# Moving the low parts of split weights and the sums of x from GpSimd to VectorE, and giving a projection's second block more PSUM banks

## The chip, the cores and the metric

The kernel runs on one core of a Trainium2 chip. The metric is the device time of one execution in microseconds. A core has five engines that each work through a queue of their own in order: TensorE (PE) multiplies matrices, VectorE (DVE), ScalarE (ACT) and GpSimd (POOL) work element by element, and SyncE (SP) issues most transfers. SBUF is the memory on the core, and matrix products land in eight PSUM banks.

## The reference, cut to what matters

The reference is one inference step of a two-layer decoder over 1024 prompt tokens and 64 sample tokens, 1024 features, all in fp32. Layer 0 mixes by retention, layer 1 by dilated window attention, and both attend to a memory as well. After the mixer of each layer:

```python
xp = deepnorm_residual(xp, mix_p @ w_out[l], ln_mix_g[l], ln_mix_b[l])
xp = deepnorm_residual(xp, swiglu_ffn(xp, w_ffn_in[l], w_ffn_out[l]), ln_ffn_g[l], ln_ffn_b[l])

def deepnorm_residual(x, h, g, b):
    return layer_norm(ALPHA * x + h, g, b)

def swiglu_ffn(x, w_in, w_out):
    gate, up = jnp.split(x @ w_in, 2, axis=-1)          # 2 x 2816 columns
    return (jax.nn.silu(gate) * up) @ w_out
```

The sample tokens go through the same lines. The change lies in the projection by `w_out` and in the FFN.

## The kernel before

**Products from halves.** Each fp32 operand is held as a high part `h` (rounded to the matrix unit's fp32r by ScalarE) and a low part `l = x - h` (a subtraction). A product is three matmuls: high by low, low by high, high by high. `halves` (L232) makes both parts of a weight piece: `acopy` (L149) on ScalarE writes `wh`, `tt` (L152) on VectorE or GpSimd writes `wl`. L149 and L152 are the lines of nearly all element-wise work in the profile, so groups are told apart by the tiles they write.

**Weights.** `plan` lists all weights in the order of use. `load_raw` fetches an entry to `raw` or `rawu` tiles by SP, two entries ahead; `emit_piece` (L237) cuts it into pieces and splits them. A ring of six `wh`/`wl` tiles holds the pieces ahead. Entries of the FFN's input (`sf`) hold a gate and an up column block of 128 (one f) and give seven pieces; entries of the FFN's output (`fo`) and of the projection (`wo`) give two each, whose lows GpSimd makes.

**Gate units.** The FFN runs over tokens in two blocks (0 to 511, and 512 to 1087), and in each over 22 f. A unit, one f, is a Strassen-like scheme with seven products instead of eight: `gates` (L746) multiplies the seven weight pieces with seven sums of x (`XH`, `XL`), in the order 0, 4, 2, 1, 3, 5, 6. Four banks `A_`, `B_`, `C_`, `D_` take them, and VectorE reads them into `v` and `up`, multiplies with ScalarE's SiLU and writes the low part of `hid`; ScalarE writes `hid`'s high part. The weight pieces need sums as well, on VectorE: `s` (gate minus up rows), `rawu` and two that overwrite `raw`. After every four f (three in the last two groups) the `fo` products of that group follow, read by VectorE into `mx`.

```python
            eng = nc.vector if j in SFD else nc.gpsimd      # SFD = (2, 6)
```

**Sums of x.** `combine_x` (L700) makes the seven sums, `x11`, `t2`, `t3`, `t1`, `x21`, `t4`, `x22`, and splits each with `put`. Of the seven lows GpSimd makes the first, third and fifth (`PUT`), and it makes the sum `t3x`. For block 1 they are made in one step of all four k (1152 columns), after the last gates of block 0, while the last `fo` products of block 0 run.

**Projection.** `out_proj` (L659) runs over two blocks; block 1 has eight m with two chunks of tokens (256 and 320), each product in one of three banks of the pool `pd`, read by VectorE at L683. The other pool, `pa`, has four banks, which the norms and the attention use.

**Order.** The code emits instructions in the order of the text, with background generators (`Streams`, `S.tick`) in between; a scheduler of the framework then sets each engine's order, so the lines of one unit are interleaved with those of others.

Of the kernel before, what the change touches and what calls it, by code (L numbers as in the profile page):

```python
# [8 lines left out]
F32 = mybir.dt.float32  # L9
F32R = mybir.dt.float32r  # L10
AF = mybir.ActivationFunctionType
ALU = mybir.AluOpType
AX = mybir.AxisListType

P = 128
# [72 lines left out]
def trunk(ctx: ExitStack, tc: tile.TileContext, A: dict, O: dict, g128, g8):  # L88
    nc = tc.nc
# [18 lines left out]
    TK = ((3,), (2, 5), (1, 3, 5), (4,))  # L108
    BG = (120, 126, 128)
    PA = (6, 4)  # L110
    PUT = (1, 3, 5)
    WIN_ = (5, 4)
    SR = (2, 1)
    SY = (2, 3)
# [1 line left out]
    done = set()  # L116
# [13 lines left out]
    def slot(shape, dt=F32, name="slot"):  # L130
        return slots.tile(shape, dt, tag="slot", name=name)

    def rt(shape, name="rt"):
        return tp.tile(shape, F32, tag="rt", name=name)

    def bank(name="bank"):
        return pa.tile([P, 512], F32, tag="pa", name=name)

    def dbank(name="pd"):
        return pd.tile([P, 512], F32, tag="pd", name=name)  # L140
# [7 lines left out]
    def acopy(out, in_, scale=1.0):  # L148
        nc.scalar.activation(out, in_, AF.Copy, scale=scale)  # L149

    def tt(out, a, b, op, eng=None):
        (eng or nc.vector).tensor_tensor(out=out, in0=a, in1=b, op=op)  # L152
# [22 lines left out]


    WI, WB, WKV = A["w_in_a"][0], A["w_in_b"][0], A["w_kv_shared"]
    SFD = (2, 6)
    UNITS = ((2, 0), (1, 0), (0, 0), (2, 1), (1, 1), (0, 1))
    plan = []  # L180

# [50 lines left out]
    def halves(src, kt, eng):  # L232

        wh = wsp.tile([P, 4, P], F32R, tag="wh", name="wh")[:, :kt]
        wl = wsp.tile([P, 4, P], F32R, tag="wl", name="wl")[:, :kt]
        acopy(wh, src)
        tt(wl, src, wh.bitcast(F32), ALU.subtract, eng)  # L237
        return wh, wl

    def emit_piece():  # L240
# [6 lines left out]
        if key[0] == "sf":  # L247
            k4 = lambda t: t.rearrange("p (k m) -> p k m", m=P)
            g1, g2, u1, u2 = (k4(t[:, o:o + 512]) for t in r[:2] for o in (0, 512))
            eng = nc.vector if j in SFD else nc.gpsimd  # L250
            if j == 0:
# [45 lines left out]
    def weights(key, ahead=None, keep=False):  # L297

        assert plan[at["next"]][0] == key, (plan[at["next"]][0], key)
        at["next"] += 1  # L300
        if not keep:
            for w in held:
                w.clear()
            held.clear()
        held.append([piece(1), piece(PA[1] if ahead is None else ahead)])
        return held[-1]

    def dense(out, w, rhs, kt=KT):

        for k in range(kt):  # L310
            rh, rl = rhs(k)
            wh, wl = (t[:, k % 4, :] for t in w[k // 4])
            mm(out, lhsT=wl, rhs=rh, start=(k == 0), stop=False)  # L313
            mm(out, lhsT=wh, rhs=rl, start=False, stop=False)  # L314
            mm(out, lhsT=wh, rhs=rh, start=False, stop=(k == kt - 1))  # L315
            if k in S.at and kt == KT:
                S.tick()
# [337 lines left out]
    def out_proj(l, ready):  # L655
        for blk in range(2):
            S.at = TK[2] if l and blk == 0 else TK[3]
            S.until(lambda: all(k in done for c in BCH[blk] for k in ready(c)), blk if l else 1)
            b0, bn = BLK[blk][0][0], sum(n for _, n in BLK[blk])  # L659
            bs = slice(b0, b0 + bn)  # L660
            parts = []
            for k in range(KT):
                if blk == 0 and k > 1:
                    h, lo = xh[:, k - 2, bs], xl[:, k - 2, bs]
                elif k % 2 == 0:
                    hs, ls = (slot([P, 2, bn], F32R, nm) for nm in ("mixh", "mixl"))
                    h, lo = hs[:, 0], ls[:, 0]
                else:
                    h, lo = hs[:, 1], ls[:, 1]
                acopy(h, mx[:, k, bs])  # L670
                tt(lo, mx[:, k, bs], h.bitcast(F32), ALU.subtract)
                parts.append((h, lo))
                tt(mx[:, k, bs], xhf[:, k, bs], xlf[:, k, bs], ALU.add, nc.gpsimd if blk else nc.vector)
            done.add(("moved", l, blk))
            sums = [None, None]
            for m in range(KT):
                w = weights(("wo", l, blk, m))
                for i, c in enumerate(BCH[blk]):
                    c0, n = CH[c]
                    ps = dbank()[:, :n]  # L680
                    dense(ps, w, lambda k: tuple(t[:, c0 - b0:c0 - b0 + n] for t in parts[k]))
                    y = mx[:, m, c0:c0 + n]
                    nc.vector.scalar_tensor_tensor(out=y, in0=y, scalar=ALPHA, in1=ps, op0=ALU.mult, op1=ALU.add)  # L683
                    sums[i] = stat_add(sums[i], m, c, nc.vector)
                    S.tick()
            for i, c in enumerate(BCH[blk]):
                S.add(norm(c, sums[i], 0, l), level=2)
            S.add(combine_x(l, blk), level=2)


# [9 lines left out]
    def combine_x(l, blk):  # L700

        yield from wait(*[("ln", 0, l, c) for c in BCH[blk]], ("gates", l, 0) if blk else ("moved", l, 1))
        c0, n = HALF[blk]
        XH, XL = x_sums(blk)
        kk = 4 if blk else 2
        tmp = (lambda nm: slot([P, 4, n], F32, nm)) if blk else (lambda nm: rt([P, 2, n], nm))
        for k in range(0, 4, kk):
            x11, x12, x21, x22 = (mx[:, o + k:o + k + kk, t:t + n] for o in (0, 4) for t in (c0, c0 + n))
            turn = [0]

            def put(i, src):
                acopy(XH[:, i, k:k + kk], src)
                turn[0] += 1
                tt(XL[:, i, k:k + kk], src, XH[:, i, k:k + kk].bitcast(F32), ALU.subtract, nc.gpsimd if turn[0] in PUT else nc.vector)

            put(0, x11)
            t1 = tmp("t1x")
            tt(t1, x12, x11, ALU.subtract)
            t2 = tmp("t2x")
            tt(t2, x22, t1, ALU.subtract)  # L720
            put(4, t2)
            yield 1
            t3 = tmp("t3x")
            tt(t3, x22, x12, ALU.subtract, nc.gpsimd)
            put(2, t3)
            put(1, t1)
            yield 1
            put(3, x21)
            t4 = tmp("t4x")
            tt(t4, x21, t2, ALU.subtract)  # L730
            yield 1
            put(5, t4)
            put(6, x22)
            yield 1
        done.add(("xsum", l, blk))
# [9 lines left out]
    def ffn(l, background):  # L745
        def gates(blk, f, last):  # L746

            n = HALF[blk][1]
            XH, XL = x_sums(blk)
            assert plan[at["next"]][0] == ("sf", l, blk, f)  # L750
            at["next"] += 1

            def prod(i, ps, start, stop):
                wh, wl = piece(PA[0])
                for k in range(4):
                    mm(ps, lhsT=wl[:, k], rhs=XH[:, i, k], start=start and k == 0, stop=False, skip_group_check=True)  # L756
                    mm(ps, lhsT=wh[:, k], rhs=XL[:, i, k], start=False, stop=False, skip_group_check=True)  # L757
                    mm(ps, lhsT=wh[:, k], rhs=XH[:, i, k], start=False, stop=stop and k == 3, skip_group_check=True)  # L758
                S.tick()
                return ps  # L760

            sets["use"] ^= 1
            A_, B_, C_, D_ = (new_bank(i)[:, :n] for i in range(4))
            v, u1, u0 = (rt([P, n], nm) for nm in ("v1", "up1", "up0"))
            hid = slot([P, 2, 2 * n], F32R, "hid")

            def result(i, u, g):

                hs = slice(i * n, i * n + n)
                tt(g, u, g, ALU.mult)  # L770
                acopy(hid[:, 0, hs], g)
                tt(hid[:, 1, hs], g, hid[:, 0, hs].bitcast(F32), ALU.subtract)

            prod(0, A_, True, True)
            acopy(v, A_)
            prod(4, B_, True, True)
            tt(v, v, B_, ALU.add)
            prod(2, C_, True, True)
            tt(u1, v, C_, ALU.add)
            prod(1, D_, True, True)  # L780
            tt(u1, u1, D_, ALU.add)
            prod(3, A_, False, True)
            nc.scalar.activation(A_, A_, AF.Silu)
            prod(5, C_, False, True)
            tt(u0, v, C_, ALU.add)
            result(0, u0, A_)
            prod(6, D_, False, True)
            if last:
                done.add(("gates", l, blk))
            tt(D_, v, D_, ALU.add)  # L790
            nc.scalar.activation(D_, D_, AF.Silu)
            result(1, u1, D_)
            return hid

        def parts(outs, gi, hid, b0):
# [739 lines left out]
    kv, kt = mkv_view(0), mkt_view(0)  # L1535
# [123 lines left out]
```

## Time and profile before

| | |
|---|---|
| median of 3 runs | 2837.92 us (2834.95 to 2838.29) |
| the profiled execution | 2834.16 us |
| its span, first to last instruction | 2832.4 us |
| mean granted TensorE clock | 0.976 |
| busy: VectorE, ScalarE, GpSimd | 1789.0, 1190.1, 1242.8 us |
| DMA, mean | 102 GB/s |

In time the span holds: memory and layer 0's mixer to 510 us, its projection to 630, its FFN to 1450 (block 1 from 1018), layer 1's mixer to 1880, its projection to 2010, its FFN to 2800 (block 1 from about 2400), and the last rows of output. A row of groups reads: line, engine, operation, tile written and tiles read, shape, count, then busy us and mean ns of one, then the idle time of the engine before them and what ended it. A row of waits reads: engine, tile and line that waited, what it waited for, then total us, times and the longest.

### The profile page before, as it was taken

Reading aid. Unit: us, or ns where it says so; the run is one execution under the profiler, and the core shown is the slowest. Engines: PE = TensorE matmul, PEld = TensorE weight load, DVE = VectorE, ACT = ScalarE, POOL = GpSimd, SP = SyncE. Lnnn points to the kernel's source line nnn. Section 1 sums busy time; section 2 is a strip of 40 time slices with the busy share of each in tenths; the row PEclk is TensorE's granted clock in tenths of the full one; section 3 lists DMA queues with packets and bytes.
Section 4 is the critical chain, followed back from the end, with each engine's and each line's share of the span. In section 5 each row is a group of like instructions: output and inputs, shape, how many; then the busy total and the mean of one; then the engine's idle time right before and its main releaser. Section 6 shows DMA issues by size and latency. Waiting matters only on the chain. (4 is left out here: it accounts for less than half of the span.)

```text
span 2832.4 us, 47793 instructions
## 1 busy us (share of the span) xinstructions
PE 2646.8 (93%) x18057; PEld 2388.7 (84%) x18057; DVE 1789.0 (63%) x3522; ACT 1190.1 (42%) x2618; POOL 1242.8 (44%) x969
## 2 busy tenths in 40 slices
PE   8999999988999979999999999988899998899997
PEld 8778888788888869999977777667888887899997
DVE  4533445477666686666684766678766657766657
ACT  4432223235444434333455545444344434433334
POOL 0012224555555665555520111136555556755546
PEclk9999999989999989999999999989899999999999
DMA  7131111323333322333332553542233333433322
GB/s 241 30 98 54 47 54 47 98 66 97 110 113 108 123 77 92 104 108 97 107 94 91 166 153 103 149 118 78 90 100 113 109 123 101 142 109 106 97 83 90
DMA packets 417815, 289.19 MB, mean 102 GB/s; under 512 B 21360, under 2 KB 403120, under 8 KB 415920
## 3 DMA queue, kind: packets, MB, share of 16 engines
q1 hardware_dynamic: 417584, 286.13, 32.9%
q8 instruction: 143, 2.34, 0.3%
q14 instruction: 88, 0.72, 0.1%
HBM read 272.25 MB, written 40.83 MB: 111 GB/s over the span
## 5 line engine op out<-in xcount | busy, mean ns | idle before, releaser
L152 POOL TENSOR_TENSOR wl<-raw,wh 128x512 fp32r<-128x512 f32 (+1 forms) x432 | 573.3, 1333 | 556.6 <-ACT wh L149 536.6
L149 ACT ACTIVATE wh<-raw 128x512 fp32r<-128x512 f32 (+1 forms) x628 | 386.4, 622 | 569.8 <-DVE raw L152 243.6
L152 POOL TENSOR_TENSOR wl<-rawu,wh 128x512 fp32r<-128x512 f32 (+1 forms) x280 | 393.9, 1414 | 197.3 <-ACT wh L149 197.2
L313 PE MATMUL pd<-xh,wl 128*128 128x512 f32 (+2 forms) x1200 | 420.3, 351 | 0.7 <-DVE t L436 0.6
L314 PE MATMUL pd<-xl,wh 128*128 128x512 f32 (+2 forms) x1200 | 408.9, 341 | 0.2 <-DVE xl L152 0.2
L315 PE MATMUL pd<-xh,wh 128*128 128x512 f32 (+2 forms) x1200 | 407.4, 340 | 0.0
L756 PE MATMUL gb<-xh,wl 128*128 128x256 f32 (+1 forms) x1232 | 362.5, 294 | 28.6 <-DVE up L152 13.4
L758 PE MATMUL gb<-xh,wh 128*128 128x256 f32 (+1 forms) x1232 | 358.2, 291 | 0.0
L757 PE MATMUL gb<-xl,wh 128*128 128x256 f32 (+1 forms) x1232 | 355.6, 289 | 0.0
L756 PE MATMUL pd<-xh,wl 128*128 128x256 f32 (+1 forms) x880 | 259.3, 295 | 30.3 <-DVE up L152 17.8
L756 PEld LDWEIGHTS gb<-xh,wl 128*128 128x128 f32 x1232 | 234.4, 190 | 35.9 <-issue 17.2
L313 PEld LDWEIGHTS pd<-xh,wl 128*128 128x128 f32 x1200 | 227.8, 190 | 36.4 <-issue 16.4
L758 PE MATMUL pd<-xh,wh 128*128 128x256 f32 (+1 forms) x880 | 256.0, 291 | 0.0
L757 PE MATMUL pd<-xl,wh 128*128 128x256 f32 (+1 forms) x880 | 253.6, 288 | 0.0
L314 PEld LDWEIGHTS pd<-xl,wh 128*128 128x128 f32 x1200 | 228.2, 190 | 25.2 <-issue 7.7
L315 PEld LDWEIGHTS pd<-xh,wh 128*128 128x128 f32 x1200 | 227.7, 190 | 24.1 <-issue 5.1
L149 ACT ACTIVATE wh<-rawu 128x512 fp32r<-128x512 f32 (+1 forms) x280 | 170.7, 612 | 167.2 <-PE pd L808 64.8
L757 PEld LDWEIGHTS gb<-xl,wh 128*128 128x128 f32 x1232 | 236.1, 192 | 0.6 <-issue 0.2
L758 PEld LDWEIGHTS gb<-xh,wh 128*128 128x128 f32 x1232 | 234.3, 190 | 0.0
L756 PEld LDWEIGHTS pd<-xh,wl 128*128 128x128 f32 x880 | 167.2, 190 | 37.0 <-issue 23.0
L152 DVE TENSOR_TENSOR raw<-raw 128x512 f32<-128x512 f32 x88 | 113.5, 1290 | 117.0 <-POOL wl L152 117.0
L806 PE MATMUL gb<-hid,wl 128*128 128x512 f32 (+2 forms) x528 | 175.0, 333 | 11.1 <-ACT hid L149 10.7
(336 smaller groups left out, 6419.4 us busy)
## 6 DMA issues: line engine op xcount, KB each, us to landing
rawu<-in_w_ffn_in_dram SPq DMA_DIRECT2D x88, 512.0 KB
raw<-in_w_ffn_in_dram SPq DMA_DIRECT2D x88, 512.0 KB
raw<-in_w_out_dram SPq DMA_DIRECT2D x32, 512.0 KB
raw<-in_w_ffn_out_dram SPq DMA_DIRECT2D x32, 512.0 KB
rawu<-in_w_ffn_out_dram SPq DMA_DIRECT2D x32, 512.0 KB
out_wins_dram<-in_cache_win_kv_g_dram SPq DMA_DIRECT2D x64, 256.0 KB
qb<-scr_q SPq DMA_DIRECT2D x64, 256.0 KB
raw<-in_w_in_a_dram SPq DMA_DIRECT2D x26, 512.0 KB
```

Of the source, the lines that this page charges most:

```text
L149: nc.scalar.activation(out, in_, AF.Copy, scale=scale)
L152: (eng or nc.vector).tensor_tensor(out=out, in0=a, in1=b, op=op)
L313: mm(out, lhsT=wl, rhs=rh, start=(k == 0), stop=False)
L314: mm(out, lhsT=wh, rhs=rl, start=False, stop=False)
L315: mm(out, lhsT=wh, rhs=rh, start=False, stop=(k == kt - 1))
L756: mm(ps, lhsT=wl[:, k], rhs=XH[:, i, k], start=start and k == 0, stop=False, skip_group_check=True)
L757: mm(ps, lhsT=wh[:, k], rhs=XL[:, i, k], start=False, stop=False, skip_group_check=True)
L758: mm(ps, lhsT=wh[:, k], rhs=XH[:, i, k], start=False, stop=stop and k == 3, skip_group_check=True)
L806: mm(ps, lhsT=wl[:, k], rhs=hid[k][:, 0, ts_], start=first, stop=False)
```

## The change

Five of the seven lows of a gate unit's weights (pieces 0, 1, 2, 4, 6) go to VectorE, two (3 and 5) stay on GpSimd. Every low that GpSimd makes, those of `fo` and `wo` too, is made in steps of two k. All lows and sums of `combine_x` go to VectorE, and block 1 is made in two steps of two k as block 0 is. In block 1 of the projection, products with odd m take a bank of `pa`. The mark that a block's gates are done moves to the end of the unit.

```diff
-    PUT = (1, 3, 5)
-    SFD = (2, 6)
+    SFD = (0, 1, 2, 4, 6)
 def halves(src, kt, eng):
-        tt(wl, src, wh.bitcast(F32), ALU.subtract, eng)
+        step = 2 if eng is nc.gpsimd else kt
+        for k in range(0, kt, step):
+            ks = slice(k, min(k + step, kt))
+            tt(wl[:, ks], src[:, ks], wh[:, ks].bitcast(F32), ALU.subtract, eng)
 def out_proj(l, ready):
-                    ps = dbank()[:, :n]
+                    ps = (bank("po") if blk and m % 2 else dbank())[:, :n]
 def combine_x(l, blk):
-        kk = 4 if blk else 2
-        tmp = (lambda nm: slot([P, 4, n], F32, nm)) if blk else (lambda nm: rt([P, 2, n], nm))
+        kk = 2
+        tmp = (lambda nm: slot([P, 2, n], F32, nm)) if blk else (lambda nm: rt([P, 2, n], nm))
-                turn[0] += 1
-                tt(XL[:, i, k:k + kk], src, XH[:, i, k:k + kk].bitcast(F32), ALU.subtract, nc.gpsimd if turn[0] in PUT else nc.vector)
+                tt(XL[:, i, k:k + kk], src, XH[:, i, k:k + kk].bitcast(F32), ALU.subtract)
-            tt(t3, x22, x12, ALU.subtract, nc.gpsimd)
+            tt(t3, x22, x12, ALU.subtract)
             tt(t4, x21, t2, ALU.subtract)
+            put(5, t4)
             yield 1
-            put(5, t4)
 def gates(blk, f, last):
             prod(6, D_, False, True)
-            if last:
-                done.add(("gates", l, blk))
             tt(D_, v, D_, ALU.add)
             nc.scalar.activation(D_, D_, AF.Silu)
             result(1, u1, D_)
+            if last:
+                done.add(("gates", l, blk))
```

The scheduler's order moves with it. First, ScalarE in layer 0 where block 1's sums of x are made (`xh` are their high parts, `gb` at L791 the second SiLU of block 0's last unit, and `hid` its result, which the `fo` products wait for). Before:

```order
L149 ACTIVATE xh<-mx 128x1152
L149 ACTIVATE xh<-t1x 128x1152
L791 ACTIVATE gb<-gb 128x256
L149 ACTIVATE xh<-t3x 128x1152
L149 ACTIVATE xh<-t2x 128x1152
L149 ACTIVATE hid<-gb 128x256
L149 ACTIVATE xh<-t4x 128x1152
```

After, the same place:

```order
L148 ACTIVATE hid<-gb 128x256
L789 ACTIVATE gb<-gb 128x256
L148 ACTIVATE xh<-t1x 128x576
L148 ACTIVATE hid<-gb 128x256
L148 ACTIVATE xh<-t2x 128x576
L148 ACTIVATE xh<-t3x 128x576
```

The last `hid` now stands behind one high part of 576 columns, where it stood behind `t3x` and `t2x` of 1152.

Second, VectorE in a gate unit of block 1 in layer 0 (`v`, `up`, `pd` and `gp` read the products or the SiLU, `s`, `rawu` and `raw` are the sums of weights, `wl` the lows). Before:

```order
L152 TENSOR_TENSOR v_10964<-v_10964,pd 128x288
L152 TENSOR_TENSOR rawu<-rawu 128x512
L152 TENSOR_TENSOR raw<-rawu,raw 128x512
L152 TENSOR_TENSOR up_10965<-v_10964,pd 128x288
L152 TENSOR_TENSOR up_10965<-up_10965,gp 128x288
L152 TENSOR_TENSOR wl<-s_11015,wh 128x512
L152 TENSOR_TENSOR up_10966<-v_10964,pd 128x288
L152 TENSOR_TENSOR pd<-up_10966,pd 128x288
L152 TENSOR_TENSOR raw<-raw 128x512
```

After:

```order
L151 TENSOR_TENSOR v_11127<-v_11127,pd 128x288
L151 TENSOR_TENSOR rawu<-rawu 128x512
L151 TENSOR_TENSOR wl<-raw,wh 128x512
L151 TENSOR_TENSOR up_11128<-v_11127,pd 128x288
L151 TENSOR_TENSOR raw<-rawu,raw 128x512
L151 TENSOR_TENSOR up_11128<-up_11128,gp 128x288
L151 TENSOR_TENSOR wl<-raw,wh 128x512
L151 TENSOR_TENSOR wl<-s_11179,wh 128x512
L151 TENSOR_TENSOR up_11129<-v_11127,pd 128x288
L151 TENSOR_TENSOR pd<-up_11129,pd 128x288
L151 TENSOR_TENSOR wl<-raw,wh 128x512
```

Three more lows stand between the readings of the products, and each waits for its `wh` on ScalarE.

More of the change, by code (lines that the diff above doesn't have):

```diff
@@ L704, in combine_x @@
         XH, XL = x_sums(blk)
-        kk = 4 if blk else 2
-        tmp = (lambda nm: slot([P, 4, n], F32, nm)) if blk else (lambda nm: rt([P, 2, n], nm))
+        kk = 2
+        tmp = (lambda nm: slot([P, 2, n], F32, nm)) if blk else (lambda nm: rt([P, 2, n], nm))
         for k in range(0, 4, kk):
             x11, x12, x21, x22 = (mx[:, o + k:o + k + kk, t:t + n] for o in (0, 4) for t in (c0, c0 + n))
-            turn = [0]
             def put(i, src):
                 acopy(XH[:, i, k:k + kk], src)
-                turn[0] += 1
-                tt(XL[:, i, k:k + kk], src, XH[:, i, k:k + kk].bitcast(F32), ALU.subtract, nc.gpsimd if turn[0] in PUT else nc.vector)
+                tt(XL[:, i, k:k + kk], src, XH[:, i, k:k + kk].bitcast(F32), ALU.subtract)
             put(0, x11)
```

## Prediction

> **What bounds the kernel now.** I read the page's busy times first, then the list of who TensorE waited for, then the order of time around the two longest waits, then the groups of instructions in one quiet gate stretch.
>
> ```profile
> PE 2646.8 (93%) x18057; PEld 2388.7 (84%) x18057; DVE 1789.0 (63%) x3522; ACT 1190.1 (42%) x2618; POOL 1242.8 (44%) x969
> ...
> PE pd L756 <- DVE up L152: 17.8, 13, 2.6
> PE pd L806 <- ACT hid L149: 15.6, 4, 12.2
> PE pd L313 <- DVE mx L683: 14.2, 6, 3.3
> PE gb L756 <- DVE up L152: 13.4, 12, 1.7
> PE gb L806 <- ACT hid L149: 10.7, 2, 10.1
> PE pd L756 <- ACT v L149: 7.2, 9, 2.6
> PE pd L756 <- POOL wl L152: 4.9, 2, 4.3
> PE gb L756 <- ACT v L149: 4.6, 8, 0.6
> PE gb L756 <- POOL wl L152: 4.6, 3, 2.6
> ```
>
> TensorE is the bound at 93%, so only its 185 us of idle time (2832.4 less 2646.8), and time at a lower clock, can be won. The rows (total, times, longest, all us) fall into three kinds that the change touches. Two single waits for `hid`, 12.2 and 10.1 us, one per layer. Six waits, 14.2 us, of the output projection for VectorE's `mx` at L683. And many short ones in the gates: `up` 31.2, `v` 11.8, POOL's `wl` 9.5, together 52.5 us. The first kind, in order of time, at the point in layer 0 where the FFN goes from its first to its second block of tokens:
>
> ```profile
> 995.37 3.05 POOL L152 TENSOR_TENSOR wl<-raw,wh 128x384 fp32r<-128x384 f32 x2
> 998.38 2.60 POOL L152 TENSOR_TENSOR t3x<-mx 128x1152 f32<-128x1152 f32 x1
> ...
> 1001.02 1.16 ACT L149 ACTIVATE xh<-t3x 128x1152 fp32r<-128x1152 f32 x1 [10.79 <-POOL t3x L152]
> ...
> 1003.14 0.36 ACT L149 ACTIVATE hid<-gb 128x256 fp32r<-128x256 f32 x1
> ...
> 1003.56 1.65 PE L806 MATMUL pd<-hid,wl 128*128 128x512 f32 x3 [12.21 <-ACT hid L149]
> ...
> 1005.43 0.63 PE L808 MATMUL pd<-hid,wh 128*128 128x512 f32 x1
> ...
> 1007.90 0.40 PE L808 MATMUL pd<-hid,wh 128*128 128x512 f32 x1
> ```
>
> GpSimd makes the sum `t3x` only at 998.38, behind its other work. ScalarE's `xh<-t3x` waits 10.79 us for it, and the `hid` that TensorE needs stands behind that on ScalarE. No arithmetic is late: a queue is. Afterwards a matmul takes 0.63 us where it takes 0.40 from 1007.9 on.
>
> **The change, part by part.** *Sums of x by VectorE, in steps of two k.* `t3x` and three of seven lows leave GpSimd, so the chain of the fence above cannot form. I count the waits, 12.2 + 10.1, and the slow clock behind them: from 1003.56 to 1007.4 at about half rate, 1.9 us, twice. That is 26 us at most. What VectorE gets instead stands in the same stage:
>
> ```profile
> 980.00:1060.00 80.00, 58.60 (x355) 52.04 (x354) 67.74 (x86) 34.63 (x65) 53.45 (x32) 0.91 0.25 78
> 2370.00:2450.00 80.00, 60.19 (x355) 54.07 (x354) 67.17 (x88) 36.21 (x67) 59.65 (x40) 0.88 0.35 116
> ...
> L152 DVE TENSOR_TENSOR lnsum<-lnsum,mx 128x512 f32<-128x512 f32 x6 | 6.0, 1000 | 0.0
> L152 DVE TENSOR_TENSOR lnsq<-lnsq,sqt 128x512 f32<-128x512 f32 x3 | 3.9, 1300 | 0.0
> L152 DVE TENSOR_TENSOR raw<-raw 128x512 f32<-128x512 f32 x3 | 3.6, 1202 | 1.7 <-POOL wl L152 1.7
> L152 DVE TENSOR_TENSOR t4x<-mx,t2x 128x1152 f32<-128x1152 f32 x1 | 3.4, 3430 | 0.0
> L152 DVE TENSOR_TENSOR xl<-mx,xh 128x1152 fp32r<-128x1152 f32 x1 | 1.3, 1346 | 0.0
> ```
>
> The windows show PE, PEld, DVE, ACT and POOL busy; VectorE works 67.7 of 80 us. Added: one sum and three lows of 1152 columns at 1.35 us (last row, the undisturbed size), 5.4 us, and three weight lows for each of about four gate units at 0.69 us (row `wl<-raw` of the next fence, less its rare disturbance), 8.3 us. Taken away: the stretching of VectorE's two-input instructions while GpSimd works. Against 0.68 us for 512 columns and 1.35 for 1152, the four stretched rows hold 1.9 + 1.9 + 1.6 + 2.1 = 7.5 us. So VectorE needs 67.7 + 13.7 - 7.5 = 74 us of a stage of 80: it limits the gain there to 6 us, or to 9 if smaller stretched groups give back some 3 us more, an estimate. **Term: 2 x -9 = -18 us; ends -26 and 0.**
>
> *Five of seven gate lows on VectorE, two on GpSimd, in halves.* A unit (one f of a block) is seven products of 12 matmuls. For block 0:
>
> ```profile
> L152 DVE TENSOR_TENSOR raw<-raw 128x512 f32<-128x512 f32 x18 | 26.4, 1466 | 26.9 <-POOL wl L152 26.9
> L152 DVE TENSOR_TENSOR wl<-s,wh 128x512 fp32r<-128x512 f32 x18 | 21.3, 1182 | 9.9 <-ACT wh L149 9.7
> L152 DVE TENSOR_TENSOR rawu<-rawu 128x512 f32<-128x512 f32 x17 | 18.0, 1056 | 0.0
> ...
> L152 DVE TENSOR_TENSOR s<-raw,rawu 128x512 f32<-128x512 f32 x17 | 13.3, 784 | 1.8 <-DMA raw<-in_w_ffn_in_dram 1.2 <-DMA rawu<-in_w_ffn_in_dram 0.6
> L152 DVE TENSOR_TENSOR wl<-raw,wh 128x512 fp32r<-128x512 f32 x17 | 12.6, 738 | 3.6 <-ACT wh L149 3.2
> L152 DVE TENSOR_TENSOR raw<-rawu,raw 128x512 f32<-128x512 f32 x17 | 11.7, 686 | 11.5 <-POOL wl L152 11.5
> ...
> L152 DVE TENSOR_TENSOR up<-v,gb 128x256 f32<-128x256 f32 x18 | 7.5, 415 | 4.4 <-PE gb L758 4.0
> ...
> L152 POOL TENSOR_TENSOR wl<-raw,wh 128x384 fp32r<-128x384 f32 x4 | 4.0, 1020 | 3.2 <-ACT wh L149 3.2
> ...
> 954.79 0.28 PE L756 MATMUL gb<-xh,wl 128*128 128x256 f32 x1
> ...
> 956.21 0.28 PE L756 MATMUL gb<-xh,wl 128*128 128x256 f32 x1
> ...
> 2576.58 1.29 POOL L152 TENSOR_TENSOR wl<-raw,wh 128x512 fp32r<-128x512 f32 x1 [1.85 <-ACT wh L149]
> ...
> 2576.65 1.77 DVE L152 TENSOR_TENSOR s<-raw,rawu 128x512 f32<-128x512 f32 x1
> 2578.46 0.69 DVE L152 TENSOR_TENSOR rawu<-rawu 128x512 f32<-128x512 f32 x1
> ```
>
> TensorE: 12 matmuls from 954.79 to 956.21, 1.42 us a product, 9.95 a unit. VectorE today: the six weight instructions, 1.47 + 1.18 + 1.06 + 0.78 + 0.74 + 0.69 = 5.9 us; nine that read the products at 0.42, 3.8; waiting for GpSimd (26.9 + 11.5)/17.5 = 2.2. That is 11.9, 1.9 us a unit more than TensorE needs; the output products after each group of units let it catch up. After the change: nine two-input instructions at 0.69 alone, 6.2, and 3.8, is 10.0. The wait for GpSimd falls away, because the lows of pieces 0 and 4, whose source VectorE overwrites, become VectorE's own. To that come collisions: the last rows show a VectorE instruction that started beside a GpSimd low and ended 0.55 us after it instead of 0.69 us after its own start. GpSimd's halves: from 1.29 us (512) and 1.02 (384) a line gives 0.75 for 256 columns, an estimate; four a unit, 3.0 us or 30% of it. Nine instructions that meet one with chance 0.3 and wait half of it add 9 x 0.3 x 0.37 = 1.0. And the three new lows wait for ScalarE's `wh` as today's do: 3.6/17 = 0.2 or 9.9/18 = 0.55 us each. I take the 0.2, since pieces 0, 1 and 4 are made six pieces ahead: 0.6. Sum 11.6, overdraft 1.6 instead of 1.9, with 0.55 2.7. GpSimd's extra start per half, 1.50 instead of 1.29 us, hides in its idle time (44% busy). The weights' transfers follow whoever frees the raw tile, now VectorE, which is no later. Of the 43.0 us of `up` and `v` in the list above I leave 8 to the stages just treated. **Term: the other 35 us shrink by a sixth, as the overdraft does, -6 us; ends -30 (all gone, with part of the `wl` waits) and +25 (overdraft 2.7 with longer products' units too).**
>
> *Projection's second block on banks of both pools.* Odd m take a bank of the other pool, so a bank comes up for reuse after five or seven products instead of three.
>
> ```profile
> 598.12 1.75 DVE L152 TENSOR_TENSOR t1x<-mx 128x512 f32<-128x512 f32 x1
> ...
> 600.25 0.41 PE L313 MATMUL pd<-mixh,wl 128*128 128x320 f32 x1 [3.28 <-DVE mx L683]
> ...
> 601.33 0.47 PE L313 MATMUL pd<-mixh,wl 128*128 128x320 f32 x1
> ```
>
> TensorE waited 3.28 us for the read-out of L683, which stood on VectorE behind sums of x stretched to 1.75 us. The six waits, 14.2 us, have no other cause in the trace, and the sums are faster too. After the wait matmuls slow from 0.30 to 0.47 us. I take all 14.2 and 3 us of the slow clock. The norm's own tiles use the same second pool and could hold it. **Term: -17 us; ends -23 and 0.** The Trainium skill ("TensorE: Matmul & The Clock Gate", What's actually happening) has the clock halve only after a whole idle window of about 3.4 us; by that rule these shorter waits would cost no clock, and this part would be -14 instead of -17. The row at 601.33 speaks against it.
>
> *Moving the mark that the gates are done* puts it behind instructions in the same unit, with no step of the background work between; 0 us.
>
> **Sum.** -18 - 6 - 17 = -41 on the profiled execution's 2834.2 us (span 2832.4 and 1.8 around it): 2793. The median of the runs is 3.7 us above that execution, so 2797.
>
> **Rivals.** *VectorE becomes the bound (slower).* It gets three lows a unit and five of the sums' instructions. Place: the gate stretches. If each of the nine two-input instructions took 1.18 us as `wl<-s` does today, and the lows waited 0.55, a unit would need 9 x 1.18 + 3.8 + 1.65 = 16.1, overdraft 6.1; in proportion to 35 us at 1.9 that is 112 us, 77 more, against 35 won elsewhere: 2838 + 42 = 2880. It decides at an overdraft near 3.8, which is 1.1 us for each of the nine. For it speaks that ScalarE's order still couples each low to VectorE; against it, that the stretched rows are stretched by GpSimd, which does less than half as much per unit. The Trainium skill ("Perfetto Trace Analysis", Optimizing Scalar/DVE Operations) advises the opposite move where VectorE is saturated, offloading to ScalarE or even GpSimd, and adds that between VectorE and GpSimd it might not help. The trace bears out the second half, with 1.77 us for 0.69.
>
> *The wait is only exchanged.* At the block change VectorE becomes the last to arrive, the 18 us do not come, and the gates gain nothing: -17, 2821. VectorE's 74 of 80 us speak for it; that the chain at 998.38 shows GpSimd's queue and not VectorE as the cause, against.
>
> *The banks do not help*, since the norm's tiles hold the second pool's four: -24, 2814.
>
> *All ends good*: -26 - 30 - 23 = -79, 2759.
>
> *Nothing measurable*: gates lose about what the rest wins, at an overdraft near 3.8: 2838.
>
> **Chances.** Forecast 0.56, own range 2780 to 2808; exchanged 0.12; banks 0.11; all good 0.08; nothing 0.06; VectorE bound 0.07. A measurement here tells 0.2% (5.7 us) from no change. Faster 0.56 + 0.12 + 0.11 + 0.08 = 0.87, within 0.2% 0.06, slower 0.07. The range leaves out the slower rival and half of the best case: 2766 to 2830.
>
> **What would show it.** Right: no `hid` wait over 3 us; no wait on `mx` of the projection; VectorE's `raw` no longer waiting for GpSimd, and its two-input rows near 0.7 to 0.85 us; VectorE busier, GpSimd well under 44%. Wrong: `up` waits above 31 us, or gate matmuls waiting for VectorE's `wl`; projection matmuls waiting for norm tiles.

## The result, and the profile after

The changed kernel takes 2723.69 us (median of 4 runs, 2718.27 to 2725.82) beside 2836.43 us of the kernel before (4 runs); the ratio is 0.9604, 95% interval 0.9582 to 0.9627. That is 113 us faster, where 41 were forecast and 79 was the best case named. The profiled execution took 2724.47 us (span 2722.7, mean clock 0.983). The lines of its page and of its list of waits that answer to those shown of before:

```profile
PE 2619.1 (96%) x18057; PEld 2374.0 (87%) x18057; DVE 1816.9 (67%) x3832; ACT 1210.6 (44%) x2632; POOL 946.3 (35%) x1129
...
PE lnm L592 <- DVE lnsum L151: 10.1, 1, 10.1
...
PE pd L756 <- DVE up L151: 3.5, 3, 2.0
PE pd L756 <- DVE wl L151: 3.3, 3, 2.6
...
PE pd L315 <- DVE mx L685: 2.9, 2, 1.5
PE pd L806 <- POOL wl L151: 2.4, 3, 1.6
...
PE gb L756 <- DVE up L151: 1.4, 3, 0.7
...
PE pd L806 <- ACT hid L148: 1.2, 3, 0.6
```

TensorE's idle time fell from 185.6 to 103.6 us (span less busy). The two waits for `hid` (12.2 and 10.1 us) are gone, the six for `mx` (14.2 us) are two of 1.5, and the waits for `up` of the same two rows went from 31.2 to 4.9 us. New is one wait of 10.1 us for `lnsum`.

One quiet stretch says where most of the time came from: groups 2 to 4 of block 0 in layer 0, first before, then after. The columns are the stretch, then the busy time of PE, PEld, DVE, ACT and POOL, the granted clock, DMA share and GB/s.

```profile
707.70:905.90 198.20, 188.43 (x1297) 174.13 (x1296) 125.17 (x205) 82.09 (x168) 114.29 (x84) 1.00 0.35 110
```

```profile
694.50:879.20 184.70, 184.70 (x1297) 173.34 (x1296) 132.23 (x240) 84.84 (x168) 76.87 (x96) 1.00 0.38 119
```

The same 1297 matmuls take 13.5 us less. TensorE was idle for 9.8 us of the stretch before (198.20 less 188.43), and its busy time was 3.7 us longer as well, some 0.3 us for each of the twelve waits: in a row each matmul adds 0.12 us, but the last one before a wait counts with its whole 0.28 us, and the first one behind it is slower (the rows at 802.35 and 804.01 below). After the change it is busy for all of the 184.70 us. VectorE does more work than before, and no wait is left.

The groups of VectorE's weight instructions in these stretches, before and after:

```profile
L152 DVE TENSOR_TENSOR raw<-raw 128x512 f32<-128x512 f32 x13 | 18.6, 1434 | 19.3 <-POOL wl L152 19.3
L152 DVE TENSOR_TENSOR wl<-s,wh 128x512 fp32r<-128x512 f32 x12 | 14.4, 1200 | 7.1 <-ACT wh L149 6.9
L152 DVE TENSOR_TENSOR rawu<-rawu 128x512 f32<-128x512 f32 x12 | 13.4, 1113 | 0.0
...
L152 DVE TENSOR_TENSOR raw<-rawu,raw 128x512 f32<-128x512 f32 x12 | 8.2, 685 | 7.7 <-POOL wl L152 7.7
```

```profile
L151 DVE TENSOR_TENSOR wl<-raw,wh 128x512 fp32r<-128x512 f32 x48 | 37.8, 787 | 9.0 <-ACT wh L148 7.8
...
L151 DVE TENSOR_TENSOR raw<-raw 128x512 f32<-128x512 f32 x12 | 9.8, 816 | 0.1
L151 DVE TENSOR_TENSOR rawu<-rawu 128x512 f32<-128x512 f32 x12 | 8.6, 719 | 0.0
L151 DVE TENSOR_TENSOR wl<-s,wh 128x512 fp32r<-128x512 f32 x12 | 8.2, 687 | 0.5 <-ACT wh L148 0.3
```

The wait for GpSimd (19.3 and 7.7 us in front of the two `raw` groups) is gone, and the three groups shown of before have come down from 1.1 to 1.4 us to between 0.69 and 0.82. Not every group has: `s` went from 0.77 to 0.85 us.

### The profile page after: what moved, and what is told of

Same layout as the page of the kernel before. It is cut to its first block, busy times and chain, and to the rows that moved or that the text cites. A ratio compares the mean times of both kernels' runs of the same rounds, so it can differ in the third digit from the quotient of the medians.

```text
span 2722.7 us, 48288 instructions
## 1 busy us (share of the span) xinstructions
PE 2619.1 (96%) x18057; PEld 2374.0 (87%) x18057; DVE 1816.9 (67%) x3832; ACT 1210.6 (44%) x2632; POOL 946.3 (35%) x1129
## 4 chain that ended last, share of the span: by engine, by line
PE 68%; DVE 11%; issue 4%; ACT 2%; DMA 2%; POOL 2%; SPq 0%; DVEq 0%; ACTq 0%; POOLq 0%
PE gb L758 5%; PE gb L756 5%; PE gb L757 5%; PE pd L315 4%; PE pd L316 4%; PE pd L317 4%; PE pd L756 4%; PE pd L758 4%; PE pd L757 4%; PE gb L806 3%; PE gb L807 3%; PE gb L808 3%; PE pd L806 3%; PE pd L807 3%; PE pd L808 3%
## 5 line engine op out<-in xcount | busy, mean ns | idle before, releaser
L151 POOL TENSOR_TENSOR wl<-rawu,wh 128x256 fp32r<-128x256 f32 (+1 forms) x560 | 444.7, 818 | 809.2 <-ACT wh L148 744.8
L151 DVE TENSOR_TENSOR wl<-raw,wh 128x512 fp32r<-128x512 f32 x460 | 343.6, 751 | 112.7 <-ACT wh L148 108.8
L756 PE MATMUL gb<-xh,wl 128*128 128x256 f32 (+1 forms) x1232 | 358.6, 291 | 3.0 <-DVE up L151 1.4
L151 POOL TENSOR_TENSOR wl<-raw,wh 128x256 fp32r<-128x256 f32 x336 | 267.2, 821 | 125.8 <-ACT wh L148 112.5
L756 PE MATMUL pd<-xh,wl 128*128 128x256 f32 (+1 forms) x880 | 257.2, 292 | 8.9 <-DVE up L151 3.5
L317 PEld LDWEIGHTS pd<-xh,wh 128*128 128x128 f32 x1200 | 227.9, 190 | 24.2 <-issue 5.1
L756 PEld LDWEIGHTS gb<-xh,wl 128*128 128x128 f32 x1232 | 233.3, 189 | 5.2 <-DVE up L151 1.5
L756 PEld LDWEIGHTS pd<-xh,wl 128*128 128x128 f32 x880 | 167.6, 190 | 10.9 <-DVE wl L151 4.3
```

## The experiments

All kernels stand in one table. Ratios are to the kernel before, timed in the same round. The scheduler orders each kernel anew, so that an edit can move other instructions as well. "Four units" is the length of four gate units of groups 2 to 4, in block 0 and block 1. The other columns are differences to before in the profiled executions, in us, cut where TensorE's first matmul of the next stage starts: both projections (271.1 before); the gate groups, block 0 complete and block 1 from its second group (1326.1); the two block changes, from the last gates of block 0 to the second group of block 1 (233.4); and the rest, mostly the mixers (1001.8). One execution stands behind each difference; the rest, which the edits hardly touch, scatters from -7 to +8, so the changed kernel's -4.8 there is not put down to any of them. The gates scatter too: po_only and sums_only, whose four units are as long as before, stand at +6.8 and +6.1 there.

| kernel | ratio [95%] | four units | projections | gates | block changes | rest |
|---|---|---|---|---|---|---|
| before | 1 | 44.3 / 46.8 | | | | |
| changed | 0.9604 [0.9582, 0.9627] | 39.9 / 44.6 | -24.2 | -57.3 | -23.4 | -4.8 |
| own_2 | 0.9862 [0.9843, 0.9882] | 41.7 / 44.6 | -6.3 | -34.8 | +0.9 | -2.1 |
| notown_5 | 0.9779 [0.9756, 0.9802] | 40.3 / 44.6 | -5.1 | -49.4 | -7.9 | -0.7 |
| own_5 | 0.9756 [0.9735, 0.9778] | 39.9 / 44.6 | -6.0 | -54.5 | -9.6 | -4.1 |
| halves_only | 0.9935 [0.9911, 0.9959] | 44.0 / 46.5 | -13.8 | -11.4 | 0.0 | +8.0 |
| own_2_halves | 0.9771 [0.9742, 0.9799] | 40.9 / 44.6 | -13.7 | -48.2 | +0.8 | -5.2 |
| po_only | 0.9952 [0.9936, 0.9967] | 44.3 / 46.8 | -17.7 | +6.8 | +1.8 | +1.8 |
| sums_only | 0.9931 [0.9914, 0.9947] | 44.4 / 46.8 | -11.3 | +6.1 | -13.1 | -3.1 |
| after_nohalves | 0.9651 [0.9630, 0.9671] | 39.9 / 44.6 | -16.7 | -56.6 | -19.8 | -2.9 |
| after_all7 | 0.9637 [0.9615, 0.9659] | 39.9 / 44.6 | -22.8 | -53.3 | -23.7 | -0.4 |
| after_4 | 0.9616 [0.9594, 0.9638] | 39.9 / 44.6 | -27.5 | -55.4 | -22.0 | -6.9 |
| after_2 | 0.9666 [0.9639, 0.9694] | 40.9 / 44.6 | -27.1 | -49.7 | -18.8 | +2.3 |
| after_lnm4 | 0.9622 [0.9607, 0.9638] | 39.9 / 44.6 | -25.7 | -57.7 | -24.6 | -1.7 |
| after_lnsum_pool | 0.9624 [0.9604, 0.9644] | 39.9 / 44.6 | -23.7 | -57.3 | -21.2 | -0.3 |
| after_put_pool | 0.9600 [0.9581, 0.9620] | 39.9 / 44.6 | -30.2 | -58.5 | -24.0 | -3.5 |

**Why the gates gained: the wait for GpSimd, or GpSimd's work.** Three theories: VectorE's wait in order for GpSimd before it overwrites a source (1); the holding up of VectorE's two-input instructions by GpSimd's (2); the halves (3). Four kernels from before, each with one edit.

```diff
-    SFD = (2, 6)
+    SFD = (0, 4)               # own_2
+    SFD = (1, 2, 3, 5, 6)      # notown_5
+    SFD = (0, 1, 2, 4, 6)      # own_5
```

> The kernel before with one edit: VectorE makes the lows of pieces 0 and 4 (whose source it overwrites itself afterwards) in place of 2 and 6; still two of seven on VectorE and five on GpSimd. Theory 1 (VectorE's wait in order for GpSimd before it overwrites a source is what cost the gate stretches): that wait of 175 us goes, and most of the 58 us that the gate stretches gained with the whole change comes here too, about 2780 to 2795 us. Theory 2 (the stretching of VectorE's two-input instructions by GpSimd's work is what cost it): GpSimd works as much as before, 2836 us within 6. Theory 3 (halves): the same, 2836.

> The kernel before with one edit: VectorE makes five lows (1, 2, 3, 5, 6), GpSimd only those of pieces 0 and 4, whose sources VectorE overwrites afterwards. Theory 1: VectorE still waits for GpSimd at every overwritten source, and has three more instructions: no gain, 2836 to 2870. Theory 2: GpSimd's gate lows fall from five to two as in the whole change, so the gates gain as there, about 2780.

> The kernel before with one edit: the split of lows of the whole change (VectorE 0, 1, 2, 4, 6), nothing else. Theories 1 and 2 both: the 58 us of the gate stretches, about 2780. Theory 3 (halves matter): clearly less, above 2800.

The fourth has only the change's edit of `halves`:

> The kernel before with one edit: each low that GpSimd makes is made in two instructions. Theory 1: no gain, since VectorE waits for the second half, up to 10 us slower (2836 to 2846). Theory 2: GpSimd works a little longer in all, 2836 within 6. Theory 3 (a short GpSimd instruction holds VectorE up for less): 15 us or more faster, below 2821.

Neither of the first two theories stands alone. With the wait gone and GpSimd's five lows kept, own_2 (2790.84 us, in theory 1's range) gains 35 us in the gates, where theory 2 said none; with the wait kept and two lows on GpSimd, notown_5 (2767.30 us) gains 49, where theory 1 said none. Together (own_5, 2759.80 us, 20 better than expected) it is 54.5, not the sum: each brings block 1 to TensorE's own pace, and there is nothing more to win. The halves alone come to 2810.43 us, which theory 3 had forecast (below 2821), but not where it looked. The quiet gates hardly move (44.0 instead of 44.3): VectorE's holds are shorter there (`raw` 1.05 us instead of 1.43), and its waits for GpSimd in front of `raw` longer (28.3 us instead of 19.3). The largest part, 13.8 us, lies in the projections, and most of it is TensorE's clock (see "Do the parts add up?").

The groups of VectorE show what was left in each. In own_2 (first) the wait is gone and the holds have stayed; in notown_5 (second, with its window of the three quiet groups) the wait has stayed, and of the holds mainly the one on `rawu`.

```profile
L152 DVE TENSOR_TENSOR rawu<-rawu 128x512 f32<-128x512 f32 x12 | 18.6, 1554 | 0.3
L152 DVE TENSOR_TENSOR raw<-raw 128x512 f32<-128x512 f32 x12 | 12.6, 1047 | 0.1
```

```profile
L152 DVE TENSOR_TENSOR rawu<-rawu 128x512 f32<-128x512 f32 x12 | 14.3, 1194 | 0.0
...
L152 DVE TENSOR_TENSOR raw<-raw 128x512 f32<-128x512 f32 x13 | 9.0, 692 | 11.8 <-POOL wl L152 11.8
...
L152 DVE TENSOR_TENSOR raw<-rawu,raw 128x512 f32<-128x512 f32 x12 | 8.2, 685 | 7.7 <-POOL wl L152 7.7
...
710.10:896.48 186.38, 185.89 (x1297) 173.39 (x1296) 131.64 (x241) 83.33 (x168) 66.22 (x48) 1.00 0.37 117
```

How a hold becomes a wait of TensorE is seen in order of time in the kernel before (start, duration, idle time in brackets):

```profile
801.70 1.28 POOL L152 TENSOR_TENSOR wl<-raw,wh 128x512 fp32r<-128x512 f32 x1 [3.30 <-ACT wh L149]
...
802.25 1.28 DVE L152 TENSOR_TENSOR rawu<-rawu 128x512 f32<-128x512 f32 x1
802.35 0.28 PE L758 MATMUL gb<-xh,wh 128*128 128x256 f32 x1
803.46 0.41 DVE L152 TENSOR_TENSOR up<-v,gb 128x256 f32<-128x256 f32 x1
...
804.01 0.36 PE L756 MATMUL gb<-xh,wl 128*128 128x256 f32 x1 [1.39 <-DVE up L152]
```

GpSimd's low ends at 802.98; VectorE's `rawu`, which began in the middle of it, ends 0.55 us after that, at 803.53. The read-out `up`, short in itself, stands behind it, and TensorE waits 1.39 us for `up` because a bank is to be used again. Of the 1.39 us the hold makes 0.6 (`rawu` takes 1.28 us instead of 0.68); what makes the other 0.8 was not taken apart. It is one instruction that comes late, on an engine that is busy for 63% of the stretch.

**Is VectorE anywhere near its limit?** That was the rival on the slow side.

```diff
-    SFD = (0, 1, 2, 4, 6)
+    SFD = (0, 1, 2, 3, 4, 5, 6)      # after_all7
+    SFD = (0, 1, 4, 6)               # after_4
```

> The changed kernel with one edit: VectorE makes all seven lows of a gate unit. Theory A (a unit's pace is TensorE's 9.95 us or VectorE's occupancy, whichever is longer): VectorE, occupied for 9.7 us of a unit in the groups 2 to 4 (132.23 us less 15.8 for the fo sums, over 12 units), gets two lows more (1.2 to 1.3), loses the collisions (0.8) and waits a little more for ScalarE: 10.8 to 11.2 us, so block 0's units lengthen by about 1 us and block 1's (11.15 on TensorE) do not: 44 units, 2765 us. Theory B (with GpSimd's gate lows gone, the collisions pay for the two lows): 2724 to 2735.

> The changed kernel with one edit: VectorE makes four lows (0, 1, 4, 6), GpSimd three. Quiet gate stretches: still TensorE's pace, 39.9 us per four units. At the block changes and in the first groups VectorE has less to do: up to 8 us faster than the changed kernel (2716) if VectorE's load is the limit there; 3 to 8 us slower if GpSimd's lows then stretch it as much as they relieve it.

```profile
696.60:881.30 184.70, 184.70 (x1297) 173.33 (x1296) 138.99 (x264) 85.05 (x168) 35.58 (x48) 1.00 0.38 119
```

This window of after_all7 covers the same three groups. With all seven lows VectorE is busy for 138.99 of 184.70 us. Its sums of the `fo` products are 16.5 us of that, so a unit takes (138.99 - 16.5)/12 = 10.2 us, more than TensorE's 9.95, and TensorE still never waits here. Theory A's rule, pace by unit, does not hold. A reading that fits is that the 22 us of `fo` products after each four units let VectorE catch up, so that the total of a group counts (46 of 61.6 us); but 0.25 us a unit is little, and the pieces held ahead could have covered it too. after_all7 comes out some 9 us behind the changed kernel by the ratios (0.9637 beside 0.9604, overlapping intervals), inside Theory B's range, and not through the quiet stretch. after_4 cannot be told from the changed kernel.

**Length of a hold, or GpSimd's total?** Pieces 0 and 4 on VectorE, with halves:

```diff
-    SFD = (2, 6)
+    SFD = (0, 4)                     # own_2_halves: before, with the edit of halves; after_2: changed kernel
```

> The kernel before with two edits: VectorE makes the lows of pieces 0 and 4, and GpSimd makes its five in halves. Theory H (what delays TensorE is the length of a single hold of VectorE in front of a read-out; beside a half it is held at most about 0.8 us instead of 1.3 to 1.7): groups 2 to 4 of block 0 fall from 41.7 us per four units to 40.0 to 40.6; with the projection's 14 us of the halves, 2765 to 2775 in all. Theory W (GpSimd's total work counts, and the halves make it longer): 41.7 us stay, 2783 to 2790.

> The changed kernel with VectorE making only the lows of pieces 0 and 4, the five others GpSimd in halves. Theory H: four units take 40.0 to 40.6 us, and VectorE is freer at the block changes: 2718 to 2735. Theory W: 41.7 us per four units, about 2745.

GpSimd's instructions are 10 per unit instead of 5 and its total work grows, yet four units fall from 41.7 to 40.9 us. In the stretch of one group TensorE's waits for `up` are one of 0.5 us in own_2_halves (763 to 825 us; second fence) where own_2 has 1.2 and 0.8 (770 to 835; first fence):

```profile
PE gb L756 <- DVE up L152: 1.2, 1, 1.2
PE pd L756 <- DVE up L152: 0.8, 1, 0.8
```

```profile
PE gb L759 <- DVE up L152: 0.5, 1, 0.5
```

This group of own_2 is its slowest; in the other two of the stretch the waits come to 1.3 and 1.2 us. So shorter holds help against more total work, as theory H says, but only to 40.9 in both kernels, just outside its 40.0 to 40.6; the rest down to 39.9 came only with fewer GpSimd instructions (own_5). Both length and number of holds count. In all, own_2_halves (2770.08 us) is in theory H's range, and after_2 (2740.36 us) is not: it lies between H's 2718 to 2735 and W's 2745.

**The projection's banks, and the sums of x,** each alone on the kernel before:

```diff
-                    ps = dbank()[:, :n]
+                    ps = (bank("po") if blk and m % 2 else dbank())[:, :n]      # po_only
```

> The kernel before with one edit: odd m of the projection's second block take a bank of the other pool. Theory A (a wait also costs the TensorE windows at half rate that follow it): the six waits for mx, 14.2 us, and in each layer some 10 us at half rate behind them go, 14.2 + 2 x 5 = 24 us, about 2805 to 2812. Theory B (the wait alone): 14 us, 2815. Theory C (the norm's tiles hold the banks): no gain, 2829.

`combine_x` as a whole as in the change, the rest as before:

> The kernel before with one edit: all sums of x and their lows by VectorE, in steps of two k. Theory A (the whole waits for hid go): 22 us and two slow windows, about 2804. Theory B (the wait is exchanged in layer 0, where in the whole change TensorE waits 10.1 us for VectorE's lnsum): about 13 us, 2816.

po_only takes 17.7 us off the projections, 8.7 of TensorE's idle time and 9.0 of its busy time. The windows before the norm, of the kernel before and of po_only (same columns as above), show that it is more than the wait:

```profile
597.70:601.10 3.40, 0.85 (x6) 0.85 (x7) 3.40 (x4) 0.63 (x1) 3.40 (x3) 1.00 0.52 154
601.10:604.50 3.40, 3.40 (x14) 3.40 (x14) 3.40 (x3) 1.78 (x3) 3.40 (x3) 0.50 0.00 0
```

```profile
597.40:600.80 3.40, 3.40 (x29) 3.40 (x28) 3.40 (x5) 0.63 (x1) 3.40 (x3) 1.00 0.51 154
600.80:604.20 3.40, 3.40 (x26) 3.40 (x26) 3.40 (x4) 1.78 (x3) 3.40 (x3) 1.00 0.00 0
```

In the kernel before a window with 0.85 us of matmuls is followed by one at clock 0.50, in which 14 matmuls pass instead of 26. In po_only neither happens. In the whole kernel's time po_only measures 0.9952, 9 to 18 us: nearer to the waits alone than to 24. sums_only is 20 us faster than the kernel before by its ratio (15 to 24), between Theory A's 25 and Theory B's 13. The trace is Theory B's, as are the block changes (-13.1): the `hid` waits of 12.2 and 10.1 us go, and in layer 0 TensorE waits 11.1 us for VectorE instead:

```profile
PE lnm L590 <- DVE lnsum L152: 11.1, 1, 11.1
```

**Do the parts add up?**

```diff
-        step = 2 if eng is nc.gpsimd else kt
+        step = kt                        # after_nohalves
```

> The changed kernel with one edit undone: GpSimd's lows in one instruction again. Theory A (the halves only shorten the holds of VectorE's read-outs in the projection, which the banks of both pools cover as well): at most 5 us slower than the changed kernel, 2724 to 2729. Theory B (the parts add up): 18 us slower, as the halves alone were faster, 2742.

after_nohalves lies between: 0.9651, some 13 us behind the changed kernel by the ratios, 7.5 of it in the projections and nothing in the gates' quiet stretches. The four parts alone (own_5, halves, sums, banks) give 69 + 18 + 20 + 14 = 121 us by their ratios; together they give 113, no difference that the intervals could show. In the projections alone they do not add up: the four come to 48.8 us and together give 24.2. TensorE's idle time there, and the time at a granted clock of 0.5, in us of the profiled executions, say why:

| kernel | idle | at clock 0.5 |
|---|---|---|
| before | 27.9 | 51.2 |
| own_5 | 27.8 | 37.5 |
| halves_only | 24.6 | 23.9 |
| sums_only | 26.0 | 27.3 |
| po_only | 19.2 | 30.7 |
| changed | 14.0 | 27.3 |

The idle time adds up: alone the parts take 0.1 + 3.3 + 1.9 + 8.7 = 14.0 us off it, and the whole change 13.9. The rest is busy time at the lower clock, and each part alone has already removed much of the same 51.2 us. How much goes differs from kernel to kernel for no reason that the runs show: the changed kernel, after_all7, after_4, after_2 and after_put_pool have 13.9 to 14.2 us idle, and 27.3, 30.7, 20.5, 20.5 and 13.7 us at 0.5. So some 8 us of the column of projections can be clock alone; own_5's -6.0 is.

**Can the new wait be taken away?** Three tries at the block change (in the first, the 4 in place of 1 is the number of products issued before `lnm`; `None` in the second gives the sum to GpSimd):

```diff
-        y0, y1, y2 = LNY[1] if calm else LNY[2 * which]
+        y0, y1, y2 = (4, 11, 2) if calm and which else LNY[1] if calm else LNY[2 * which]   # after_lnm4
-        sums[i] = stat_add(sums[i], m + q, c, nc.vector)
+        sums[i] = stat_add(sums[i], m + q, c, nc.vector if blk else None)   # after_lnsum_pool, with after_lnm4's line
-        tt(XL[:, i, k:k + kk], ..., ALU.subtract)
+        tt(XL[:, i, k:k + kk], ..., ALU.subtract, nc.gpsimd if blk and i in (3, 5, 6) else nc.vector)   # after_put_pool
```

> The changed kernel with one number changed: in layer 0's block change the norm's first matmul (lnm), for which TensorE waits 10.1 us at 985.10, is issued three products later. If TensorE's order is the limit there: 4 to 9 us faster than the changed kernel, 2715 to 2720. If VectorE's load is (its instructions stand back to back from 966 to 986), the products behind wait instead: no gain, 2724.

> The changed kernel with lnm three products later and, in layer 0's block change, the norm's sum (lnsum, seven adds of 512 columns, 4.2 us of VectorE from 966 to 986) on GpSimd, which is idle for 20 of those 30 us. If VectorE's load is the limit there: 4 us faster than the changed kernel, 2720. If GpSimd's adds stretch VectorE's own: no difference.

> The changed kernel with three of the seven lows of x's sums in block 1 (those of x21, t4 and x22, the last that the gates use) on GpSimd, six instructions in each block change, 3.6 us of VectorE. If VectorE's load is the limit: 2 x 3 us faster, 2718. If a read-out or a product then waits for GpSimd: slower, up to 2735.

None can be told from the changed kernel: 0.9622, 0.9624 and 0.9600 beside 0.9604, intervals overlapping. In the changed kernel VectorE's instructions stand back to back in front of the late `lnm`; from 977 to 981 three take 1.21 to 1.28 us instead of 0.68 to 0.75, beside a GpSimd run of 4.37 us:

```profile
975.72 4.37 POOL L151 TENSOR_TENSOR wl<-rawu,wh 128x256 fp32r<-128x256 f32 x4 [10.20 <-ACT wh L148]
```

```profile
977.10 1.28 DVE L151 TENSOR_TENSOR xl<-t1x,xh 128x576 fp32r<-128x576 f32 x1
978.31 1.21 DVE L151 TENSOR_TENSOR lnsum<-lnsum,mx 128x512 f32<-128x512 f32 x1
979.44 1.27 DVE L151 TENSOR_TENSOR xl<-t3x,xh 128x576 fp32r<-128x576 f32 x1
...
984.37 0.68 DVE L151 TENSOR_TENSOR lnsum<-lnsum,mx 128x512 f32<-128x512 f32 x1
```

With `lnm` later, the gate products wait instead (4.3 us once, for VectorE's `wl`); work given back to GpSimd wins no time. Whether a lighter VectorE would win any, with the work given to neither, was not tried and stays open.

## Why the prediction was wrong

**Gate lows: this step failed.** The term, an overdraft of VectorE per unit that shrinks only from 1.9 to 1.6 us, was -6 us with -30 as its good end. The gates measured -57.3, and -54.5 for the split of lows alone, and after the change VectorE has no overdraft: it is busy for (132.23 - 16.5)/12 = 9.6 us a unit beside TensorE's 9.95. Three things in the term were off.

First, the sum of VectorE's unit, 11.6 us, added up durations. Back to back they overlap, as these rows of the changed kernel show:

```profile
759.83 0.69 DVE L151 TENSOR_TENSOR wl<-raw,wh 128x512 fp32r<-128x512 f32 x1
760.44 0.68 DVE L151 TENSOR_TENSOR rawu<-rawu 128x512 f32<-128x512 f32 x1
761.04 0.41 DVE L151 TENSOR_TENSOR up<-v,gb 128x256 f32<-128x256 f32 x1
761.37 0.69 DVE L151 TENSOR_TENSOR raw<-rawu,raw 128x512 f32<-128x512 f32 x1
```

A 0.69 us instruction is followed 0.61 us after its start, a 0.41 us one after 0.33. Eighteen of them are 18 x 0.08 = 1.4 us less than their durations: about 10.2 instead of 11.6, of which 0.6 were waits for ScalarE, so 9.6 busy, as measured. The 11.9 of before shrinks too, by 15 x 0.08 = 1.2, to 10.7. By the prediction's own reasoning the overdraft would then have gone from about 0.75 to 0.25, by two thirds, and the term would have been about -23 instead of -6 (an estimate). The Trainium skill ("Perfetto Trace Analysis", Optimizing Scalar/DVE Operations) says of VectorE's fixed data-access overhead, about 60 ns on SBUF, that the profiled latency shows about twice that, since half of it overlaps with the next instruction. The trace agrees, with 0.08 us of overlap; the prediction drew on that section for another sentence and left this one out of its sum. The collisions were sized too high as well: by the prediction's own row a held instruction ends 0.55 us after GpSimd's, so a wait of 0.37 us makes it 0.23 us longer, 0.6 us a unit instead of 1.0; the groups of the changed kernel show 0.7.

Second, the reasoning itself, a loss in proportion to the overdraft per unit, was the wrong model. In notown_5 VectorE's unit is 9.6 us busy (131.64 less 16.5, over 12) and 1.6 waiting for GpSimd, 11.2 in all, where it was 9.1 and 2.2, 11.3, before: hardly another overdraft, and yet four units fall from 44.3 to 40.3 us. after_all7 has 10.2 us a unit and not one wait in the quiet groups. What stopped TensorE were single late read-outs, as the one at 803.46 behind a held instruction, and those the change removed as good as wholly (waits for `up` from 31.2 to 4.9 us). The prediction saw both the wait (26.9 + 11.5 us) and the collisions, and then melted them into an average.

Third, the size. The price was taken from the listed waits for `up` and `v`, less 8 us. In the three groups shown the waits are 9.8 us, and the loss was 13.5: around each wait the busy time grows too, 3.7 us in all. Measured against TensorE's own length, 4 x 9.95 = 39.8 us for four units that took 44.3, the loss in the quiet groups could have been read off the profile of before.

**Block changes:** -18 forecast, -23.4 measured, in the term's ends (-26, 0). That it came so near is luck in part: the sums alone give -13.1, and the gate lows, which the term had as a cost alone, another -9.6. The rival "only exchanged" came true for the single wait in layer 0, where the new one of 10.1 us took the place of one of 12.2 (sums_only gains 2.8 us in that block change); there the 74 us of VectorE's 80 had pointed at it. With the whole change layer 0's block change still gains 9.4 us, and layer 1's 14.0.

**Projections:** -17 forecast, -24.2 measured, just past the good end (-23). The banks alone measured -17.7, but that this is the forecast number is luck: the idle time fell by 8.7 us where 14.2 were taken (two waits for `mx` of 2.3 us stay in po_only), and the clock gave 9.0 where 3 were taken. That waits are followed by slow matmuls held; how much that costs is chance in part, as the clock column above shows. Of the rest, the halves give 7.5 us (after_nohalves); the other edits were not taken out one by one. The rival that the norm's tiles hold the banks fell.

**The mark** shows no wait; it was not run alone. **VectorE as the bound** fell, even with seven lows. What would show it held in all four right signs: no `hid` wait over 3 us, `raw` no longer waiting for GpSimd, two-input rows at 0.69 to 0.85 us, GpSimd at 35%. For `mx` two waits of 1.5 us are left, where none was to be. Of the wrong signs one appeared: gate matmuls wait for VectorE's `wl`, 3.3 us in three waits at L756 (row above) and 0.4 in one more, none of them in the quiet groups. And the sums give VectorE four instructions, as the term has it, not five, as the rival says.

## What to carry to other kernels

Price a bound engine's loss in a stage by the stage's length less that engine's undisturbed length, not by the waits that are listed. When it waits for a short read-out, look at the longest instruction that can stand in front of that read-out in its queue, and at what can hold it; an engine 63% busy can be late at every turn. Take occupancy from start to start, since a sum of durations overstates it. And before an edit is credited with a difference in a stage, part it into idle time and time at a lower clock.

## What the runs showed of the hardware

A VectorE instruction of 512 columns with both inputs in SBUF that begins beside one of GpSimd's lows ends 0.55 us after that one's end, whatever was left of it (0.35 us for 320 columns and 0.61 for 576, in the changed kernel): a hold, not a sharing of speed. The Trainium skill ("SBUF — State Buffer", SBUF: two separate sides) states an exclusive lock, for VectorE instructions with two SBUF inputs, for which the loser fully blocks; the trace agrees (802.98 and 803.53 above). Read-outs with one input in PSUM are not held: `up<-v,gb` of 256 columns takes 0.42 us in the kernel before, beside GpSimd and away from it. They can still come late, when a held instruction stands in front of them in VectorE's queue.

TensorE's granted clock changes on a grid of 3.41 us in every trace here. In the 16 profiled executions of this case (515 to 2700 us), a window at full rate with under 40% of matmul time was followed by half rate in all 152 cases, with 40 to 50% in 58 of 79, with 50 to 60% in 19 of 125, and above 60% in 8 of 9491. Full rate came back after a half-rate window over 90% busy in 225 of 257 cases, and from under 70% in none of 86. The Trainium skill ("TensorE: Matmul & The Clock Gate", What's actually happening) gives this window, but names an idle window as what halves the rate; here a window with 0.85 of 3.40 us busy did it. So a wait of 2 us can cost another 1.7 behind it (half of one window), or nothing, by where it falls.
